# Two weight subtractions moved into the gating chain, and GpSimd's table products paced by the block, in the feed-forwards of a hybrid decoder

## Chip, cores and metric

The kernel runs on one core of one Trainium2 chip. The metric is the device time of one launch in microseconds (us).

## What is computed

A decoder trunk of two layers over 256 positions of width 1024, all in float32. Each layer adds half a feed-forward, a token mixer and half a second feed-forward to `x`; a last RMSNorm ends it.

```python
def swiglu(h, w_gate, w_up, w_down):
    return (jax.nn.silu(h @ w_gate) * (h @ w_up)) @ w_down

for l in range(2):
    x = x + 0.5 * swiglu(rmsnorm(x, norm_w[l, 0]), ffn_w_gate[l, 0], ffn_w_up[l, 0], ffn_w_down[l, 0])
    h = rmsnorm(x, norm_w[l, 1])
    m = even_mixer(h, ...) if l % 2 == 0 else odd_mixer(h, ...)
    x = x + m
    x = x + 0.5 * swiglu(rmsnorm(x, norm_w[l, 2]), ffn_w_gate[l, 1], ffn_w_up[l, 1], ffn_w_down[l, 1])
return rmsnorm(x, final_norm_w)
```

The hidden width of a feed-forward is 2816, that is 22 blocks of 128. The even mixer is spatial gating beside sparse attention; the odd mixer is causal pooling beside a diagonal state-space layer, for which tables (powers of a complex number, products of them with the matrices B and C, phases) have to be made from the parameters. There are four feed-forwards, called f = 0 to 3 here; the even mixer stands between 0 and 1, the odd one between 2 and 3.

## The kernel before

Products in float32 are made from two halves: a tile is rounded to `fp32r` (the high half, `h`) and the rest is kept as the low half (`l`), and three matmuls add high x high, low x high and high x low. The weights come as a stream of units of 128 x 1024 in the order in which TensorE wants them. One `raw` load on SP's queue (L87) brings two units; for each unit ScalarE makes `wh` (L97) and VectorE makes `wl`, the rest (L98). Three `raw` buffers and seven pairs `wh`, `wl` rotate. `used()` tells that a unit is done with and splits further units (`split_to`) up to six ahead; a further load is issued behind the subtraction that frees its buffer (`load_to`).

A feed-forward (`ffn(f)`) works block by block. For block j, `proj` multiplies the two units of gate and up weights into the PSUM bank `gu[j]` (48 matmuls, L125, L127, L132), and `chain(j)` makes the gated product: VectorE scales it (`e`, L252), ScalarE takes the silu (`s`, L255), VectorE multiplies (`h`, L257), ScalarE rounds (`hh`, L260), VectorE keeps the rest (`hl`, L261). `down(j)` multiplies one unit of down weights by `hh` and `hl` into the four banks `y` (24 matmuls, L114 to L116: the first two need `hh`, the third `hl`).

The order on every engine is the order of the program; nothing reorders it. Blocks 0 to 2 are opened together (`opening`); from j = 3 on a block is `proj(j)`, `chain(j)`, `down(j-1)`, and after the loop `down(21)` stands alone, with the update of `x` and the preparation of the next stage (`done`, L738 and `xprep2`, `xlow`) behind it. As `used()` is called twice within `proj`, VectorE's order in a block is `wl`, `wl`, `e`, `h`, `hl`, and one more `wl` after `down`.

`jobs[f, j]` holds work for the mixers that is issued ahead of block j. For the odd mixer (`odd_prep`), f = 0 has small operations of 32 to 288 columns on GpSimd; f = 1 and the start of f = 2 have the products `mul2`, each three GpSimd operations of 512 columns (L923 to L925), one `mul2` a block: two for `bbar` and eight for `wtw` in blocks 3 to 12 of f = 1, two scalings and the load of `cq` in block 13, five for `vt` in blocks 14 to 18, and four in blocks 3 to 6 of f = 2. `turn_w` (four TensorE transposes and a copy by ScalarE) needs all of `wtw` and `cols` and `taps` need `vt`. `bounce` brings a table through DRAM by DMAs on GpSimd's queue (`kd`, `toep`), and `phase` makes the phases in blocks 15 to 18 of f = 2. A copy of one column of `hl[2]` into `pace` (L289) holds GpSimd back until the first loop block of f = 0, 1 and 2; behind it GpSimd runs through its queue as fast as it can.

Of the kernel before, what the change touches and what calls it, by code (L numbers as in the profile page):

```python
# [7 lines left out]
F32 = mybir.dt.float32  # L8
# [4 lines left out]
OP = mybir.AluOpType  # L13
# [8 lines left out]
AHEAD = 6  # L22
# [35 lines left out]
def trunk(ctx, tc, a, out):  # L58
# [12 lines left out]
    def bank(i, name):  # L71
        return ps.tile([128, 512], F32, tag=f"bank{i}", name=name)

    v2 = lambda t: t.rearrange("p (a b) -> p a b", a=2)
    V, S, P, G = nc.vector, nc.scalar, nc.tensor, nc.gpsimd
# [2 lines left out]
    where = {u: i for i, u in enumerate(units)}  # L78
    nchunk = len(units) // 2
    raw, halves = {}, {}  # L80
    at = {"load": 0, "split": 0, "used": 0, "hold": False}

    def load_to(n):
        while at["load"] < min(n, nchunk):
            c = at["load"]
            raw[c] = wts.tile([128, 2, 1024], F32, tag="raw", name="raw", bufs=3)
            nc.sync.dma_start(raw[c], a["ws"][c].rearrange("p (u n) -> p u n", u=2))  # L87
            at["load"] += 1

    def split_to(n):  # L90
        while at["split"] < min(n, len(units)):
            i = at["split"]
            load_to(i // 2 + 1)
            src = raw[i // 2][:, i % 2]
            h = wts.tile([128, 1024], F32R, tag="wh", name="wh", bufs=AHEAD + 1)
            lo = wts.tile([128, 1024], F32R, tag="wl", name="wl", bufs=AHEAD + 1)
            S.copy(h, src)  # L97
            V.tensor_tensor(lo, src, h.bitcast(F32), op=OP.subtract)  # L98
            halves[i] = (h, lo)
            at["split"] += 1  # L100
            load_to((i + 1) // 2 + 3)

    def unit(u):
        i = where[u]
        assert i <= at["used"] + AHEAD and i < at["split"], (u, i, at)
        return halves[i]

    def used(n=1):
        at["used"] += n
        if not at["hold"]:  # L110
            split_to(at["used"] + AHEAD)
# [6 lines left out]
    def pairs(todo, half, ks=range(4)):  # L118
        for k in ks:
            for name, o in todo:  # L120
                h, lo = unit(("w", name, half))
                for s in range(2):
                    c = slice(256 * k + 128 * s, 256 * k + 128 * s + 128)
                    os = o[:, T * s:T * s + T]
                    P.matmul(os, h[:, c], xh[:, 4 * half + k], start=half == 0 and k == 0 and s == 0, stop=False,  # L125
                             skip_group_check=True)
                    P.matmul(os, lo[:, c], xh[:, 4 * half + k], start=False, stop=False, skip_group_check=True)  # L127
            for name, o in todo:
                h, lo = unit(("w", name, half))
                for s in range(2):  # L130
                    c = slice(256 * k + 128 * s, 256 * k + 128 * s + 128)
                    P.matmul(o[:, T * s:T * s + T], h[:, c], xl[:, 4 * half + k], start=False,  # L132
                             stop=half == 1 and k == 3, skip_group_check=True)

    def opening(todo, extra=None):
        at["hold"] = False
        split_to(5 if extra else at["used"] + AHEAD)
        n = 4 if extra else 1
        pairs(todo, 0)
        pairs(todo, 1, range(n))  # L140
        stats()
        used(2)
        pairs(todo, 1, range(n, 4))
        if extra:
            pairs([extra], 0)
        spread()

    def proj(name, o):
        pairs([(name, o)], 0)
        used()  # L150
        pairs([(name, o)], 1)
        used()
# [86 lines left out]
    def rows_out(u, y, ah, al, first, last, done=None):  # L239
        h, lo = unit(u)  # L240
        for d in range(ND):
            c = slice(128 * d, 128 * d + 128)
            mm3(y[d // 2][:, T * (d % 2):T * (d % 2) + T], h[:, c], lo[:, c], ah, al, first and d % 2 == 0, last)
            if done and d % 2:
                done(d // 2, y[d // 2])

    def ffn(f, after):
        gu, hh, hl, y = {}, {}, {}, {}

        def chain(j):  # L250
            e = v2(wk.tile([128, 512], F32, tag="e", name="e", bufs=3))
            V.tensor_tensor(e, gu[j].rearrange("p (a b) -> p a b", a=2), rb[:, None, :].to_broadcast([128, 2, T]),  # L252
                            op=OP.mult)
            s = wk.tile([128, T], F32, tag="s", name="s")
            S.activation(s, e[:, 0], AF.Silu)  # L255
            h = wk.tile([128, T], F32, tag="h", name="h")
            V.tensor_tensor(h, s, e[:, 1], op=OP.mult)  # L257
            hh[j] = wk.tile([128, T], F32R, tag="hh", name="hh", bufs=3)
            hl[j] = wk.tile([128, T], F32R, tag="hl", name="hl", bufs=3)
            S.copy(hh[j], h)  # L260
            V.tensor_tensor(hl[j], h, hh[j].bitcast(F32), op=OP.subtract)  # L261

        def down(j, done=None):
            if j == 0:
                for i in range(4):
                    y[i] = bank(i, "y")
            rows_out(("d", f, j), y, hh[j], hl[j], j == 0, j == NM - 1, done)

        for j in range(2):
            gu[j] = bank(4 + j, "gu")  # L270
        gu[2] = bank(6, "gu")
        extra = None if f else ((f, 2), gu[2])
        opening([((f, j), gu[j]) for j in range(2)], extra)
        chain(0)
        chain(1)
        used(2)
        if not extra:
            pairs([((f, 2), gu[2])], 0)
        used()
        pairs([((f, 2), gu[2])], 1)  # L280
        used()
        chain(2)
        down(0)
        used()
        down(1)
        used()
        for j in range(3, NM):
            if j == 3 and f < 3:
                G.tensor_copy(pace, hl[j - 1].bitcast(F32)[:, 0:1])  # L289
            for job in jobs.get((f, j), ()):  # L290
                job()
            gu[j] = bank(4 + j % 3, "gu")
            proj((f, j), gu[j])
            chain(j)
            down(j - 1)
            used()
        down(NM - 1, after)
        used()
# [415 lines left out]
    for half in range(2):  # L714
        for u in (2 * half, 2 * half + 1):
            halves[u] = tuple(wts.tile([128, 1024], F32R, tag=t, name=t, bufs=AHEAD + 1) for t in ("wh", "wl"))
        for k in range(4):
# [4 lines left out]
            for u in range(2):  # L722
                c = slice(256 * k, 256 * k + 256)
                h, lo = halves[2 * half + u]
# [33 lines left out]
    def odd_prep():  # L758
# [147 lines left out]
        def put(f, j0, per, todo):  # L906
            for i, t in enumerate(todo):
                jobs.setdefault((f, j0 + i // per), []).append(t)
# [40 lines left out]
        def turn_w(q):  # L949
            p = bank(7, "wt")  # L950
            for n in range(4):
                P.transpose(p[:, 128 * n:128 * n + 128], tw["w"][:, 4 * q + n].rearrange("p c i -> p (c i)"), ident)
            S.copy(uu[:, 4 * q:4 * q + 4], p.rearrange("p (a b) -> p a b", a=4))
# [6 lines left out]
        def taps(r4):  # L960
            kc = tw[r4]
            if r4 % 2 == 0:
                tw["p"] = bank(7, "kt")
            p = tw["p"].rearrange("p (r e n) -> p r e n", r=2, e=2)
            for e in range(2):
                for q in range(4):
                    g = 2 * (4 * r4 + q)
                    P.matmul(p[32 * q:32 * q + 32, r4 % 2, e], bbar[:, 0, g:g + 2].rearrange("p g c -> p (g c)"),
                             kc[:, 2 * q + e].rearrange("p n c -> p (n c)"), start=True, stop=True,
                             skip_group_check=True)  # L970
            if r4 % 2:
                S.copy(kk[:, :, r4 - 1:r4 + 1].rearrange("p e r n -> p r e n"), p)
# [51 lines left out]
            f(w[:, :, 0:n], e[:, :, 1:m], bc(c), MUL)  # L1024
            f(e[:, :, m + 1:2 * m], u[:, :, 0:n], w[:, :, 0:n], ADD)

        put(1, 13, 1, [lambda q=q: turn_w(q) for q in range(8)])
        put(2, 8, 1, [lambda r=r: taps(r) for r in range(4)] + [diag, bounce, phase_open])
        put(2, 7, 1, [lambda r=r: cols(r) for r in range(4)])
        put(2, 15, 1, [lambda m=m: phase(m) for m in (2, 4, 8, 16)])  # L1030
# [209 lines left out]
            run(g_)  # L1240

    jobs = {}
    tw = {}
    prm = cst.tile([128, 3, 32], F32, name="prm")
    sgn = cst.tile([128, 1], F32, name="sgn")
# [4 lines left out]
    for t_, n_ in ((prm, "prm"), (sgn, "sgn")):  # L1250
        nc.gpsimd.dma_start(t_, a[n_])
    prep = odd_prep()
    next(prep)
    ffn(0, step(1, 0.5))
    even(step(2, 1.0))
    evp_cm.__exit__(None, None, None)
# [17 lines left out]
    odd_open()  # L1274
    next(prep, None)
    ffn(1, step(3, 0.5))
    ffn(2, step(4, 0.5))
    odd(step(5, 1.0))
    ovp_cm.__exit__(None, None, None)
# [20 lines left out]
    for h2 in (1, 0):  # L1300
        for t in range(2):
            n = 2 * t + h2
# [157 lines left out]
```

## Time and profile before

| | |
|---|---|
| median of 3 runs | 996.04 us (995.7 to 997.96) |
| the profiled execution | 998.27 us, span 996.6 us |
| TensorE matmuls busy | 963.1 us, 97% of the span |
| VectorE, ScalarE, GpSimd busy | 69%, 49%, 31% |
| granted clock of TensorE, mean | 0.988 |

The span is the time from the first to the last instruction of the profiled execution. The feed-forwards lie at about 24 to 200 us (f = 0), 331 to 531 us (f = 1), 531 to 724 us (f = 2) and 795 to 985 us (f = 3). Matmuls are pipelined and the ends of their records are modelled, so their start times are what tells when TensorE waited.

### The profile page before, as it was taken

Reading aid. Unit: us, or ns where it says so; the run is one execution under the profiler, and the core shown is the slowest. Engines: PE = TensorE matmul, PEld = TensorE weight load, DVE = VectorE, ACT = ScalarE, POOL = GpSimd, SP = SyncE. Lnnn points to the kernel's source line nnn. Section 1 sums busy time; section 2 is a strip of 40 time slices with the busy share of each in tenths; the row PEclk is TensorE's granted clock in tenths of the full one; section 3 lists DMA queues with packets and bytes.
Section 4 is the critical chain, followed back from the end, with each engine's and each line's share of the span. In section 5 each row is a group of like instructions: output and inputs, shape, how many; then the busy total and the mean of one; then the engine's idle time right before and its main releaser. Section 6 shows DMA issues by size and latency. Waiting matters only on the chain.

```text
span 996.6 us, 19296 instructions
## 1 busy us (share of the span) xinstructions
PE 963.1 (97%) x8075; PEld 938.1 (94%) x8075; DVE 685.2 (69%) x943; ACT 484.6 (49%) x741; POOL 310.8 (31%) x439
## 2 busy tenths in 40 slices
PE   8999999998788999999999999999999999999997
PEld 7999999997677998899999999999998999999997
DVE  6766666597755788886558875658687687566663
ACT  6544444477444553445544444434454655444442
POOL 1399989010020259860001622296010000000001
PEclk9999999999889999999999999999999999999998
DMA  7665664533212544546443464595543546545521
GB/s 259 254 223 183 231 234 178 211 134 141 107 43 85 182 170 173 190 177 243 167 172 127 179 233 176 197 254 194 187 134 127 206 150 231 207 175 185 196 86 43
DMA packets 32856, 175.47 MB, mean 176 GB/s; under 512 B 7792, under 2 KB 10032, under 8 KB 12928
## 3 DMA queue, kind: packets, MB, share of 16 engines
q1 hardware_dynamic: 29696, 166.21, 46.2%
q0 software_dynamic: 2496, 7.41, 2.7%
q8 instruction: 63, 1.03, 0.4%
q10 hardware_dynamic: 576, 0.62, 0.2%
q14 instruction: 25, 0.20, 0.1%
HBM read 172.12 MB, written 2.10 MB: 175 GB/s over the span
## 4 chain that ended last, share of the span: by engine, by line
PE 78%; DVE 11%; ACT 4%; issue 4%; POOL 1%; DMA 1%; SPq 1%; ACTq 0%; POOLq 0%; DVEq 0%
PE gu L125 14%; PE gu L127 14%; PE gu L132 14%; PE y L116 8%; PE y L114 8%; PE y L115 8%; DVE wl L98 5%; DVE h L257 1%; ACT wh L97 1%; DVE e L252 1%; ACT pr L545 1%; DMA raw<-in_ws 1%; ACT s L255 1%; DVE pr L557 1%; PE ms L219 1%
## 5 line engine op out<-in xcount | busy, mean ns | idle before, releaser
L98 DVE TENSOR_TENSOR wl<-raw,wh 128x1024 fp32r<-128x1024 f32 x308 | 399.1, 1330 | 116.7 <-ACT wh L97 116.4
L125 PE MATMUL gu<-xh,wh 128*128 128x256 f32 x1408 | 365.6, 282 | 1.4 <-ACT wh L725 1.4
L127 PE MATMUL gu<-xh,wl 128*128 128x256 f32 x1408 | 364.3, 282 | 0.6 <-DVE wl L726 0.4
L97 ACT CAST wh<-raw 128x1024 fp32r<-128x1024 f32 x308 | 310.4, 1048 | 92.0 <-PE gu L132 42.7
L132 PE MATMUL gu<-xl,wh 128*128 128x256 f32 x1408 | 275.9, 281 | 0.0
L125 PEld LDWEIGHTS gu<-xh,wh 128*128 128x128 f32 x1408 | 266.0, 189 | 3.0 <-ACT wh L725 2.1
L127 PEld LDWEIGHTS gu<-xh,wl 128*128 128x128 f32 x1408 | 265.1, 188 | 2.0 <-DVE wl L726 1.7
L132 PEld LDWEIGHTS gu<-xl,wh 128*128 128x128 f32 x1408 | 213.7, 188 | 0.0
L114 PE MATMUL y<-hh,wh 128*128 128x256 f32 x704 | 198.4, 282 | 4.6 <-ACT hh L260 4.6
L116 PE MATMUL y<-hl,wh 128*128 128x256 f32 x704 | 199.0, 283 | 1.5 <-DVE hl L261 1.5
L115 PE MATMUL y<-hh,wl 128*128 128x256 f32 x704 | 198.3, 282 | 0.0
L255 ACT ACTIVATE s<-e 128x256 f32<-128x256 f32 x88 | 36.8, 418 | 240.1 <-DVE e L252 240.1
L114 PEld LDWEIGHTS y<-hh,wh 128*128 128x128 f32 x704 | 132.6, 188 | 5.8 <-ACT hh L260 5.8
L116 PEld LDWEIGHTS y<-hl,wh 128*128 128x128 f32 x704 | 132.5, 188 | 3.0 <-DVE hl L261 2.9
L115 PEld LDWEIGHTS y<-hh,wl 128*128 128x128 f32 x704 | 132.6, 188 | 0.0
L197 POOL TENSOR_TENSOR sq<-sq 128x512 f32<-128x512 f32 x10 | 13.7, 1366 | 255.9 <-ACT sq L195 187.8
L252 DVE TENSOR_TENSOR e<-gu,rb 128x512 f32<-128x512 f32 x88 | 60.5, 688 | 31.7 <-PE gu L132 30.7
L257 DVE TENSOR_TENSOR h<-s,e 128x256 f32<-128x256 f32 x88 | 47.9, 544 | 48.3 <-ACT s L255 48.3
L261 DVE TENSOR_TENSOR hl<-h,hh 128x256 fp32r<-128x256 f32 x88 | 41.2, 468 | 41.7 <-ACT hh L260 41.7
L260 ACT CAST hh<-h 128x256 fp32r<-128x256 f32 x88 | 35.8, 407 | 53.7 <-DVE h L257 53.7
L747 POOL TENSOR_SCALAR sq<-x,gw 128x256 f32<-128x256 f32 x4 | 3.6, 917 | 184.2 <-DVE x L738 184.2
L775 POOL TENSOR_TENSOR sq<-sq 128x64 f32<-128x64 f32 (+1 forms) x120 | 59.5, 515 | 3.6
(334 smaller groups left out, 1134.5 us busy)
## 6 DMA issues: line engine op xcount, KB each, us to landing
raw<-in_ws SPq DMA_DIRECT2D x154, 1024.0 KB, 4.8
toep<-kd POOLq DMA_DIRECT2D x8, 256.0 KB, 8.4
raw<-in_ws SPq DMA_DIRECT2D x4, 256.0 KB, 4.0
raw<-in_ws SPq DMA_DIRECT2D x2, 512.0 KB, 8.0
w<-in_w POOLq DMA_DIRECT2D x1, 1024.0 KB, 5.2
bnd<-in_bnd POOLq DMA_DIRECT2D x1, 544.0 KB, 5.4
x<-in_x SPq DMA_DIRECT2D x4, 128.0 KB, 3.3
x<-in_x SPq DMA_DIRECT2D x2, 256.0 KB, 7.3
```

Source lines behind the costliest of these rows:

```text
L97: S.copy(h, src)
L98: V.tensor_tensor(lo, src, h.bitcast(F32), op=OP.subtract)
L114: P.matmul(o, h, ah, start=first, stop=False, skip_group_check=True)
L115: P.matmul(o, lo, ah, start=False, stop=False, skip_group_check=True)
L116: P.matmul(o, h, al, start=False, stop=last, skip_group_check=True)
L125: P.matmul(os, h[:, c], xh[:, 4 * half + k], start=half == 0 and k == 0 and s == 0, stop=False, skip_group_check=True)
L127: P.matmul(os, lo[:, c], xh[:, 4 * half + k], start=False, stop=False, skip_group_check=True)
L132: P.matmul(o[:, T * s:T * s + T], h[:, c], xl[:, 4 * half + k], start=False, stop=half == 1 and k == 3, skip_group_check=True)
L252: V.tensor_tensor(e, gu[j].rearrange("p (a b) -> p a b", a=2), rb[:, None, :].to_broadcast([128, 2, T]), op=OP.mult)
L255: S.activation(s, e[:, 0], AF.Silu)
L257: V.tensor_tensor(h, s, e[:, 1], op=OP.mult)
L775: steps.append(lambda: G.tensor_tensor(o, p, q, op=op))
```

## The change

Within `proj` of the loop blocks (j from 3 on) the subtraction `wl` isn't issued with its `wh` any more but noted in `lows`. `chain(j)` issues one of the two behind the silu, ahead of `h`, and one behind `hh`, ahead of `hl`; what is left is issued after the chain. `load_to` goes with the subtraction. ScalarE's order stays. The copy into `pace` is issued ahead of the jobs of more blocks: block 3 of f = 0 as before, blocks 3 to 18 of f = 1, and blocks 3 to 6 and 15 to 18 of f = 2. `turn_w` starts at block 14 instead of 13.

```diff
@@ split_to @@
             S.copy(h, src)
-            V.tensor_tensor(lo, src, h.bitcast(F32), op=OP.subtract)
             halves[i] = (h, lo)
             at["split"] += 1
+            lows.append((i, src, h, lo))
+            if not at["wait"]:
+                lower()
+
+    def lower(n=None):
+        while lows and n != 0:
+            i, src, h, lo = lows.pop(0)
+            V.tensor_tensor(lo, src, h.bitcast(F32), op=OP.subtract)
             load_to((i + 1) // 2 + 3)
+            n = n and n - 1
...
@@ chain @@
             S.activation(s, e[:, 0], AF.Silu)
+            lower(1)
             h = wk.tile([128, T], F32, tag="h", name="h")
             V.tensor_tensor(h, s, e[:, 1], op=OP.mult)
...
             S.copy(hh[j], h)
+            lower(1)
             V.tensor_tensor(hl[j], h, hh[j].bitcast(F32), op=OP.subtract)
...
@@ ffn @@
         for j in range(3, NM):
-            if j == 3 and f < 3:
+            if (f, j) in paced:
                 G.tensor_copy(pace, hl[j - 1].bitcast(F32)[:, 0:1])
             for job in jobs.get((f, j), ()):
                 job()
             gu[j] = bank(4 + j % 3, "gu")
+            at["wait"] = True
             proj((f, j), gu[j])
+            at["wait"] = False
             chain(j)
+            lower()
             down(j - 1)
             used()
...
-        put(1, 13, 1, [lambda q=q: turn_w(q) for q in range(8)])
+        put(1, 14, 1, [lambda q=q: turn_w(q) for q in range(8)])
...
+    paced = {(0, 3)} | {(1, j) for j in range(3, 19)} | {(2, j) for j in (3, 4, 5, 6, 15, 16, 17, 18)}
```

## Rows read from the trace of the kernel before

**Rows 1.** The page: busy time of the engines (us, share of the span, instructions), and the issues of the weight loads (count, KB each, us from issue to landing).

```profile
PE 963.1 (97%) x8075; PEld 938.1 (94%) x8075; DVE 685.2 (69%) x943; ACT 484.6 (49%) x741; POOL 310.8 (31%) x439
...
raw<-in_ws SPq DMA_DIRECT2D x154, 1024.0 KB, 4.8
```

**Rows 2.** Busy time in windows of 25 us, in the order PE, PEld, DVE, ACT, POOL, each with its number of instructions, then the granted clock, the DMA share and GB/s: a window of f = 0 and two of f = 1.

```profile
75.00:100.00 25.00, 25.00 (x213) 25.00 (x212) 16.66 (x18) 11.33 (x15) 24.38 (x51) 1.00 0.52 184
...
375.00:400.00 25.00, 22.56 (x182) 21.54 (x180) 21.59 (x16) 8.07 (x12) 24.21 (x16) 1.00 0.50 180
400.00:425.00 25.00, 23.68 (x193) 23.08 (x194) 21.56 (x18) 10.80 (x15) 21.10 (x16) 1.00 0.53 196
```

**Rows 3.** Who waited for whom, TensorE only (us in total, times, longest): first in 345 to 440 us, then in 540 to 600 us.

```profile
PE y L114 <- ACT hh L260: 2.8, 4, 0.7
PE y L116 <- DVE hl L261: 1.2, 5, 0.3
...
PE y L114 <- ACT hh L260: 0.6, 1, 0.6
PE y L116 <- DVE hl L261: 0.4, 1, 0.4
```

**Rows 4.** Timeline of TensorE in f = 1 (start us, duration us, what; in brackets the idle time before it and what ended it): the beginning of the first and the fifth stalled `down`.

```profile
370.29 0.28 PE L114 MATMUL y<-hh,wh 128*128 128x256 f32 x1
...
370.86 0.39 PE L116 MATMUL y<-hl,wh 128*128 128x256 f32 x1 [0.17 <-DVE hl L261]
...
410.86 0.39 PE L116 MATMUL y<-hl,wh 128*128 128x256 f32 x1 [0.20 <-DVE hl L261]
```

**Rows 5.** The same in f = 2.

```profile
568.88 0.28 PE L114 MATMUL y<-hh,wh 128*128 128x256 f32 x1
...
579.05 0.39 PE L116 MATMUL y<-hl,wh 128*128 128x256 f32 x1 [0.38 <-DVE hl L261]
```

**Rows 6.** Timeline of VectorE in the stalled blocks of f = 1 (equal neighbours are merged, with their count).

```profile
358.95 8.07 DVE L98 TENSOR_TENSOR wl<-raw,wh 128x1024 fp32r<-128x1024 f32 x4 [0.53 <-ACT wh L97]
...
370.07 0.73 DVE L261 TENSOR_TENSOR hl<-h,hh 128x256 fp32r<-128x256 f32 x1 [0.47 <-ACT hh L260]
371.01 6.03 DVE L98 TENSOR_TENSOR wl<-raw,wh 128x1024 fp32r<-128x1024 f32 x3 [0.21 <-ACT wh L97]
...
378.19 1.43 DVE L257 TENSOR_TENSOR h<-s,e 128x256 f32<-128x256 f32 x1 [0.54 <-ACT s L255]
...
381.04 6.02 DVE L98 TENSOR_TENSOR wl<-raw,wh 128x1024 fp32r<-128x1024 f32 x3 [0.22 <-ACT wh L97]
```

**Rows 7.** Timelines of the last two blocks of f = 0: VectorE, then TensorE (the beginning of `down(21)`).

```profile
184.12 1.22 DVE L98 TENSOR_TENSOR wl<-raw,wh 128x1024 fp32r<-128x1024 f32 x1 [1.36 <-ACT wh L97]
185.83 0.69 DVE L252 TENSOR_TENSOR e<-gu,rb 128x512 f32<-128x512 f32 x1 [0.49 <-PE gu L132]
...
188.91 2.36 DVE L98 TENSOR_TENSOR wl<-raw,wh 128x1024 fp32r<-128x1024 f32 x2 [0.53 <-ACT wh L97]
...
194.36 0.69 DVE L252 TENSOR_TENSOR e<-gu,rb 128x512 f32<-128x512 f32 x1 [0.47 <-PE gu L132]
195.60 0.43 DVE L257 TENSOR_TENSOR h<-s,e 128x256 f32<-128x256 f32 x1 [0.55 <-ACT s L255]
196.50 0.42 DVE L261 TENSOR_TENSOR hl<-h,hh 128x256 fp32r<-128x256 f32 x1 [0.47 <-ACT hh L260]
...
198.59 0.68 DVE L738 SCALAR_TENSOR_TENSOR x<-y,x 128x512 f32<-128x512 f32 x1
...
197.01 0.28 PE L114 MATMUL y<-hh,wh 128*128 128x256 f32 x1
...
197.24 0.28 PE L116 MATMUL y<-hl,wh 128*128 128x256 f32 x1
```

**Rows 8.** Timeline of VectorE in a block of f = 2 without GpSimd.

```profile
585.59 3.50 DVE L98 TENSOR_TENSOR wl<-raw,wh 128x1024 fp32r<-128x1024 f32 x3 [0.45 <-ACT wh L97]
```

**Rows 9.** GpSimd in f = 1: timeline of the copy into `pace`, the first product, a short one, the last one for `wtw` and the last one for `vt`; then a group of its products in 358 to 440 us (count, busy us, mean ns, idle us before).

```profile
358.48 0.19 POOL L289 COPY pace<-hl 128x1 f32<-128x1 f32 x1 [19.63 <-DVE hl L261]
358.63 1.06 POOL L923 TENSOR_TENSOR gt<-bq,turn 128x512 f32<-128x512 f32 x1
...
390.52 1.24 POOL L924 TENSOR_TENSOR gt<-bbar,pw 128x512 f32<-128x512 f32 x1
...
408.10 1.30 POOL L925 TENSOR_TENSOR wtw<-gt 128x512 f32<-128x512 f32 x1
...
437.52 2.16 POOL L925 TENSOR_TENSOR vt<-gt 128x512 f32<-128x512 f32 x1
...
L925 POOL TENSOR_TENSOR wtw<-gt 128x512 f32<-128x512 f32 x8 | 13.9, 1737 | 0.6
```

**Rows 10.** The weight loads in f = 2: timeline of SP's queue (issues) and of ScalarE, and the landing times of the loads in 640 to 690 us.

```profile
647.33 0.33 SPq L87 DMA_DIRECT2D raw<-in_ws  x1
655.94 0.33 SPq L87 DMA_DIRECT2D raw<-in_ws  x1
...
660.93 1.99 ACT L97 CAST wh<-raw 128x1024 fp32r<-128x1024 f32 x2
668.05 1.05 ACT L97 CAST wh<-raw 128x1024 fp32r<-128x1024 f32 x1 [5.13 <-DMA raw<-in_ws]
...
DMA to landing us min/median/max: 4.7/6.2/12.0
```

More of the change, by code (lines that the diff above doesn't have):

```diff
@@ L80, in trunk @@
     raw, halves = {}, {}
-    at = {"load": 0, "split": 0, "used": 0, "hold": False}
+    at = {"load": 0, "split": 0, "used": 0, "hold": False, "wait": False}
+    lows = []
     def load_to(n):
@@ L97, in split_to @@
             S.copy(h, src)
-            V.tensor_tensor(lo, src, h.bitcast(F32), op=OP.subtract)
             halves[i] = (h, lo)
             at["split"] += 1
+            lows.append((i, src, h, lo))
[5 more added lines that the diff above has]
+            V.tensor_tensor(lo, src, h.bitcast(F32), op=OP.subtract)
             load_to((i + 1) // 2 + 3)
+            n = n and n - 1
     def unit(u):
         i = where[u]
-        assert i <= at["used"] + AHEAD and i < at["split"], (u, i, at)
+        assert i <= at["used"] + AHEAD and i < at["split"] - len(lows), (u, i, at)
         return halves[i]
```

## Prediction, made before the change was run

> **What bounds the kernel now.** I read the page's busy table first: TensorE's matmuls cover 97% of the span and VectorE 69% [rows 1]. An average hides where the missing part lies, so I went to the windows of 25 us [rows 2]. A window of a feed-forward in which TensorE never waits holds 213 matmuls (75 to 100 us). In the second feed-forward one holds 182 and one 193, and exactly there GpSimd is busy for 21 to 24 of 25 us and VectorE for 21.6; the granted clock is 1.00 throughout, so this isn't a slower TensorE but a waiting one. The list of who waited for whom says for what: in 345 to 440 us TensorE waits for `hh` and `hl`, the last two tiles of the gating chain, and in 540 to 600 us once more for each [rows 3].
>
> The start times give the loss exactly. A block (`proj(j)`, then `down(j-1)`) takes 8.53 us where TensorE sets the pace: `e` starts at 185.83 and 194.36 [rows 7]. The first stalled `down` starts at 370.29 and could have had its first matmul with `hl` 0.24 us later; that of the fifth starts at 410.86, where 370.53 + 4 x 8.53 = 404.65 would do [rows 4]: 6.2 us lost in the second feed-forward. In the third, 568.88 + 8.53 + 0.24 = 577.65 stands against 579.05 one block on: 1.4 us [rows 5]. Together **7.6 us**, and no change to this loop can win more there.
>
> Why is the chain late? VectorE's timeline [rows 6]: from one `wl` group at 371.01 to the next at 381.04 is 10.03 us, with three `wl` (6.03), `e`, `h` (1.43), `hl` (0.73) and three idle gaps of 0.54 + 0.47 + 0.22 = 1.23 us; so it is busy for 8.80 us of each block, and a block cannot take less than 10.03. Undisturbed, three `wl` in a row take 3.50 us and `h` and `hl` 0.43 [rows 7, 8]. The difference goes with GpSimd: its products run without a pause from 358.63 on, and those of L925 last 1.74 us in the mean where an undisturbed one has 1.30 [rows 9]. Both engines lengthen each other.
>
> **The change, part by part.**
>
> *(a) Two `wl` go into the chain.* VectorE's order in a block was `wl`, `wl`, `e`, `h`, `hl`, `wl`; it becomes `e`, `wl`, `h`, `wl`, `hl`, `wl`. No instruction is added. Where VectorE is behind, the two gaps (0.54 and 0.47 us) are filled: 1.0 us per block won. Where it is not behind (most blocks), the chain gets longer instead. The step from one VectorE start to the next with no wait between is 1.14 us for `wl` (2.36 - 1.22) [rows 7, 8]; for `h` I take 0.35 and for `e` 0.61, their durations less the same overlap of 0.08. From `e`'s start to `hl`'s end: 0.61 + 1.14 + 0.35 + 1.14 + 0.42 = 3.66 us, where 194.36 to 196.92 were 2.56 [rows 7]. In the loop that costs nothing: `hl` of block j is wanted only a whole block later (8.53 us), and that block hides it. The `wl` itself moves by up to 4.8 us (one block's second ends at 188.91 + 2.36 = 191.27; behind the `e` of 194.36 it ends at 196.11 [rows 7]), and is wanted two blocks later.
>
> The loads move with it, since a `raw` load leaves SP's queue only when the subtraction has freed its buffer. Five units lie between: the load issued at 647.33 feeds the `wh` at 660.93, 13.6 us later; 8.8 us remain after the change [rows 10]. Landing takes 4.8 us in the median of the page and 12.0 us once, beside the `toep` transfers [rows 1, 10]. That one is issued at 655.94 and already holds ScalarE until 668.05, without a wait of TensorE; it belongs to the third `wl` of a block, which moves by only 1.1 us. I take nothing: a landing of 12.0 us against the 8.8 left would bring a `wh` 3.2 us late, and TensorE wants it only two blocks on; should ScalarE's wait hold the chain instead, 3.2 us is the bound.
>
> *(b) The last block of a feed-forward.* Here the cover is gone: after `proj(21)` only `down(20)` stands before the `down(21)` that wants this very `hl`. Before, `hl` ends at 196.92 and the matmul that needs it starts at 197.24: 0.32 us to spare [rows 7]. With 3.66 us it ends at 198.02, the matmul follows 0.06 us later (as 370.07 + 0.73 and 370.86 show [rows 4, 6]): 198.08 - 197.24 = **0.84 us of stall**. `hh` ends at 196.98 and is in time for 197.01. The first three feed-forwards have this, as units of the next stage are still being split; the fourth has none left to split. 3 x 0.84 = **2.5 us**. TensorE opens the next stage at once, so nothing takes it back; the `x` update behind it moves by less (last `wl` from 197.60 + 0.35 = 197.95 on, `x` at 199.09 and not 198.59 [rows 7]: 0.5 us), so 3 x 0.5 = 1.5 us is the low bound. That `wl` lasts 1.22 us where a wait precedes it gives the high one: 3 x 1.0 = 3.0 us.
>
> [...]
>
> *(c) GpSimd's products paced.* Each paced block puts a copy of one column (0.19 us [rows 9]) ahead of that block's jobs; it waits for the `hl` of the block before, and all later GpSimd work queues behind it: the products, the load of `cq`, the copies of `cols`; `turn_w` and `taps` on TensorE wait for those (d). One block then has three products; so far the ten `mul2` of blocks 3 to 12, 30 products, ran from 358.63 to 409.40 [rows 9], that is 5.9 per 10.03 us. What do three cost? VectorE's undisturbed block is 0.61 + 3 x 1.14 + 0.35 + 0.42 = 4.80 us, so 3.73 us of 8.53 are to spare. From the contended block, (8.80 - 4.80) / 5.9 = 0.68 us per product, three 2.0 us; at most their whole undisturbed length, 1.06 + 1.24 + 1.30 = 3.6 us [rows 9]. Both fit: no paced block has VectorE as its bound, and as the products start with `hl`'s end, most fall into VectorE's idle time before the next `e`. So I take **all 7.6 us** as won; kept back are at worst the first stalls of each feed-forward, 370.53 to 370.86, 0.3 us each. The first loop block has four `wl` (8.07 us from 358.95 [rows 6]); two now follow `e`, which can start near 363.0 instead of behind all four. So `hl` ends, with every operation as long as under products (0.61 + 2.01 + 1.43 + 2.01 + 0.73), by 369.8, against 370.53.
>
> [...]
>
> *(d) Later needs.* The tables end later (358.5 + 15 x 8.53 + 3.6 = about 490 us instead of 439.7 [rows 9]); `turn_w` starts one block later, a whole block after its last product, and its eight blocks are as long at 14 to 21 as at 13 to 20. In the third feed-forward the last product ends near the end of block 6, `taps` needs it at block 8. Nothing.
>
> **Sum.** -7.6 + 2.5 = -5.1 us. The profiled execution took 998.27 us (span 996.6); it would become 993.2 and the span 991.5. It lies 2.2 us above the median of the runs, 996.04; against that I forecast 990.9, **991 us**.
>
> **Rivals.**
> 1. *The tail costs nothing* (the copy `hh` or the queue hides it, or the next stage takes it back): 996.0 - 7.6 = 988.4. Against it: only 0.32 us to spare. Chance 0.08.
> 2. *Half of the stalls stay*, because products meet the longer chain where `wl`, `h` and `hl` now stand in a row: each paced block then pays somewhat, -3.8 + 2.5: 994.7. For it: `h` at 1.43 us under products. Chance 0.13.
> 3. [...] GpSimd does the same products, and if each holds VectorE wherever it falls, the lost 7.6 us come back spread over the paced blocks, and the tails are added: 996.0 + 2.5 = 998.5. It decides from 3.73 / 3 = 1.24 us of VectorE per product on; the rows give 0.68 on average, and 1.0 for `h`. Chance 0.07.
> 4. *The change does nothing*: late `raw` loads hold `wh`, then `s` and the whole chain behind it, and take as much as is won: 996. For it only the one landing of 12.0 us. Chance 0.05.
>
> **How the numbers follow.** The forecast has 0.67, with its own range 989.5 to 993 (tails 1.5 to 3.0, 0.6 of stalls kept, and the runs' own scatter). Two in ten left out give 988.0 to 995.5, which takes in rivals 1 and 2. What tells from no change is 0.2%, 2.0 us, so "faster" ends at 994.05: the forecast, rival 1 and a third of rival 2, 0.79; same 0.13; slower 0.08.
>
> **What would show it.** TensorE's waits for `hh` and `hl` between 345 and 600 us gone, 213 matmuls in each window less the transposes; three new waits for `hl` of about 0.8 us at the ends of the first three feed-forwards; between `e` and `h` a `wl` and no idle; GpSimd's products in groups of three with pauses. Wrong would be: `wl` still near 2.0 us in all three places of a block, TensorE waits in paced blocks after 440 us, or ScalarE's `wh` waiting for `raw`.

## The result and the profile after

The changed kernel takes 991.42 us (median of 4 runs, 990.87 to 992.38), the kernel before beside it 996.9 us (4 runs, 995.7 to 997.96): the ratio is 0.9944 with a 95% interval of [0.9932, 0.9956], 4.4 to 6.8 us less. The forecast was 991.0. The time came out as foretold, and the stalls went where they were expected to go; but the experiments show that one of the two halves of the change, the new order, does nearly all of it alone, while the prediction had rested the claim that all 7.6 us go on the other, the pacing. That it hit to 0.4 us is in part luck: it counted 5.1 us down from a median of 996.04, and 5.5 us were measured from 996.9. Lines of `kernel.py` are nine to fourteen further on now: `wl` is L108, `e` L261, `s` L264, `h` L267, `hh` L270, `hl` L272, `pace` L300, `down` L123 to L125, the products L937 to L939.

The busy table and two groups of the page of the changed kernel (count, busy us, mean ns, idle time before), to be held against [rows 1]:

```profile
PE 959.7 (97%) x8075; PEld 936.7 (95%) x8075; DVE 631.5 (64%) x943; ACT 485.4 (49%) x741; POOL 294.0 (30%) x461
...
L108 DVE TENSOR_TENSOR wl<-raw,wh 128x1024 fp32r<-128x1024 f32 x308 | 382.0, 1252 | 14.9 <-ACT wh L98 14.9
...
L300 POOL COPY pace<-hl 128x1 f32<-128x1 f32 x25 | 25.0, 1001 | 151.5 <-DVE hl L272 151.5
```

VectorE has as many instructions as before and is busy for 53.7 us less; GpSimd has 22 more (the copies into `pace`) and is busy for 16.8 us less all the same. So less time is lost between these two. The windows of f = 1 in the same columns as [rows 2] show what TensorE got of it: 214 matmuls where there were 182 and 193, and VectorE and GpSimd busy for little over half of the time.

```profile
375.00:400.00 25.00, 25.00 (x214) 25.00 (x213) 14.29 (x18) 11.34 (x15) 13.14 (x12) 1.00 0.50 184
400.00:425.00 25.00, 25.00 (x214) 25.00 (x213) 13.84 (x19) 10.92 (x15) 12.93 (x13) 1.00 0.52 189
```

Who waited for whom, TensorE only, from 345 to 600 us; this is all that is left of [rows 3], and it is the tail of f = 1:

```profile
PE y L125 <- DVE hl L272: 0.5, 1, 0.5
```

A paced block on VectorE, then on GpSimd (start us, duration us, what; in brackets the idle time before it and what ended it):

```profile
386.80 0.69 DVE L261 TENSOR_TENSOR e<-gu,rb 128x512 f32<-128x512 f32 x1 [3.72 <-PE gu L141]
387.41 1.22 DVE L108 TENSOR_TENSOR wl<-raw,wh 128x1024 fp32r<-128x1024 f32 x1
388.54 0.42 DVE L267 TENSOR_TENSOR h<-s,e 128x256 f32<-128x256 f32 x1
388.88 1.22 DVE L108 TENSOR_TENSOR wl<-raw,wh 128x1024 fp32r<-128x1024 f32 x1
390.01 0.42 DVE L272 TENSOR_TENSOR hl<-h,hh 128x256 fp32r<-128x256 f32 x1
390.39 1.23 DVE L108 TENSOR_TENSOR wl<-raw,wh 128x1024 fp32r<-128x1024 f32 x1
395.33 0.69 DVE L261 TENSOR_TENSOR e<-gu,rb 128x512 f32<-128x512 f32 x1 [3.71 <-PE gu L141]
```

```profile
390.50 1.16 POOL L300 COPY pace<-hl 128x1 f32<-128x1 f32 x1 [3.95 <-DVE hl L272]
391.62 1.06 POOL L937 TENSOR_TENSOR gt<-bbar,pw 128x512 f32<-128x512 f32 x1
392.64 1.06 POOL L938 TENSOR_TENSOR gt<-bbar,pw 128x512 f32<-128x512 f32 x1
393.77 1.30 POOL L939 TENSOR_TENSOR wtw<-gt 128x512 f32<-128x512 f32 x1
```

The gaps between `e`, `h` and `hl` are filled, a block of VectorE is 4.82 us (386.80 to 391.62), and the three products lie wholly in VectorE's idle time, each as long as an undisturbed one.

Where the time went, stage by stage. The table is worked out from the start times of `e`: from the first `e` of a feed-forward to that of its last block, and from that to the first `e` of the next feed-forward, which holds the tail and, after f = 0 and f = 2, a mixer. The last four columns belong to the experiments.

| us | before | changed | order only | pace only | old tail | behind chain |
|---|---|---|---|---|---|---|
| f = 0, first `e` to last | 167.46 | 167.46 | 167.47 | 167.45 | 167.51 | 167.53 |
| f = 1 | 180.02 | 173.56 | 173.89 | 177.11 | 173.57 | 174.67 |
| f = 2 | 174.70 | 173.18 | 173.19 | 173.18 | 173.19 | 173.19 |
| f = 3 | 170.12 | 170.13 | 170.12 | 170.13 | 170.13 | 170.13 |
| tail of f = 1, next opening | 18.56 | 19.25 | 19.25 | 18.56 | 18.57 | 20.21 |
| tail of f = 2, odd mixer | 90.82 | 91.45 | 91.37 | 91.13 | 90.86 | 92.89 |
| tail of f = 0, even mixer | 150.97 | 149.68 | 149.89 | 149.26 | 149.00 | 152.51 |

The stalls removed are 6.46 (f = 1) + 1.52 (f = 2) = 7.98 us. Two tails cost 0.69 and 0.63 us; the third is hidden in the even mixer, whose time differs by 1.55 us between two executions of the very same changed kernel (149.68 here, 151.23 in the repeat below), so that profiled spans alone can't be compared to a microsecond. If the third is taken like the other two, which is an estimate, the gain by the stages is some 6.0 us; the runs give 5.5, within 4.4 to 6.8.

### The profile page after: what moved, and what is told of

Same layout as the page of the kernel before. It is cut to its first block, busy times and chain, and to the rows that moved or that the text cites. A ratio compares the mean times of both kernels' runs of the same rounds, so it can differ in the third digit from the quotient of the medians.

```text
span 989.2 us, 19297 instructions
## 1 busy us (share of the span) xinstructions
PE 959.7 (97%) x8075; PEld 936.7 (95%) x8075; DVE 631.5 (64%) x943; ACT 485.4 (49%) x741; POOL 294.0 (30%) x461
## 4 chain that ended last, share of the span: by engine, by line
PE 87%; DVE 6%; ACT 2%; issue 2%; DMA 1%; POOL 1%; SPq 1%; ACTq 0%; POOLq 0%; DVEq 0%
PE gu L134 16%; PE gu L136 16%; PE gu L141 16%; PE y L125 9%; PE y L124 9%; PE y L123 9%; DVE wl L108 2%; DMA raw<-in_ws 1%; ACT pr L559 1%; DVE pr L571 1%; PE ms L228 0%; PE sc L547 0%; PE glu L125 0%; PE zc L164 0%; PE zd L134 0%
## 5 line engine op out<-in xcount | busy, mean ns | idle before, releaser
L108 DVE TENSOR_TENSOR wl<-raw,wh 128x1024 fp32r<-128x1024 f32 x308 | 382.0, 1252 | 14.9 <-ACT wh L98 14.9
L261 DVE TENSOR_TENSOR e<-gu,rb 128x512 f32<-128x512 f32 x88 | 60.8, 690 | 256.9 <-PE gu L141 255.7
L125 PE MATMUL y<-hl,wh 128*128 128x256 f32 x704 | 198.6, 282 | 1.6 <-DVE hl L272 1.6
L123 PE MATMUL y<-hh,wh 128*128 128x256 f32 x704 | 198.2, 282 | 1.2 <-ACT hh L270 1.2
L264 ACT ACTIVATE s<-e 128x256 f32<-128x256 f32 x88 | 36.8, 418 | 204.4 <-DVE e L261 204.3
L125 PEld LDWEIGHTS y<-hl,wh 128*128 128x128 f32 x704 | 132.5, 188 | 2.4 <-DVE hl L272 2.4
L123 PEld LDWEIGHTS y<-hh,wh 128*128 128x128 f32 x704 | 132.6, 188 | 1.6 <-ACT hh L270 1.4
L270 ACT CAST hh<-h 128x256 fp32r<-128x256 f32 x88 | 35.8, 407 | 85.5 <-DVE h L267 85.5
L300 POOL COPY pace<-hl 128x1 f32<-128x1 f32 x25 | 25.0, 1001 | 151.5 <-DVE hl L272 151.5
L789 POOL TENSOR_TENSOR sq<-sq 128x64 f32<-128x64 f32 (+1 forms) x120 | 53.3, 463 | 3.6
L267 DVE TENSOR_TENSOR h<-s,e 128x256 f32<-128x256 f32 x88 | 39.4, 448 | 8.2 <-ACT s L264 8.2
```

Source lines behind the costliest of these rows:

```text
L123: P.matmul(o, h, ah, start=first, stop=False, skip_group_check=True)
L125: P.matmul(o, h, al, start=False, stop=last, skip_group_check=True)
L789: steps.append(lambda: G.tensor_tensor(o, p, q, op=op))
```

## Experiments

**The changed kernel once more.** No edit.

> The changed kernel itself once more, as the measure for the other three on the same chip: 5.1 to 5.5 us below before by the sum and by the first runs.

Measured: 991.49 us (990.07 to 991.92), ratio 0.9943 [0.9931, 0.9954]; f = 1 took 173.57 us, f = 2 173.18.

**The order alone.** The subtractions stay in the chain, the pacing is taken out, and `turn_w` starts at block 13 as before.

```diff
-        put(1, 14, 1, [lambda q=q: turn_w(q) for q in range(8)])
+        put(1, 13, 1, [lambda q=q: turn_w(q) for q in range(8)])
...
-    paced = {(0, 3)} | {(1, j) for j in range(3, 19)} | {(2, j) for j in (3, 4, 5, 6, 15, 16, 17, 18)}
+    paced = {(0, 3), (1, 3), (2, 3)}
```

> Only the new order of VectorE's queue: the two subtractions stand in the chain, but GpSimd is held back once per feed-forward, as before. My theory (both parts remove stalls, the tails cost 2.5 us): the two idle gaps of 1.0 us per stalled block go, VectorE's contended block falls from 10.03 to about 8.8 us against TensorE's 8.53, so some 0.3 us per block are kept over five to nine blocks, 1.5 to 2.5 of the 7.6 us; with the three tails the time is 2.6 to 3.6 us below before. Rival (pacing alone removes the stalls, the order only costs): 0 to 3 us above before. Rival (the order alone does it all): 5.1 us below before, as the whole change.

Measured: 991.49 us (990.18 to 992.16), ratio 0.9945 [0.9934, 0.9957]: as fast as the whole change. My theory missed (2.6 to 3.6 us below before), and its second rival, that the order alone does it all, came true. f = 1 keeps 0.33 us of its stalls, f = 2 none. VectorE, one block of f = 1 and the next `e`; then the window of 375 to 400 us:

```profile
379.72 0.68 DVE L261 TENSOR_TENSOR e<-gu,rb 128x512 f32<-128x512 f32 x1
380.32 1.48 DVE L108 TENSOR_TENSOR wl<-raw,wh 128x1024 fp32r<-128x1024 f32 x1
381.73 1.28 DVE L267 TENSOR_TENSOR h<-s,e 128x256 f32<-128x256 f32 x1
382.93 2.33 DVE L108 TENSOR_TENSOR wl<-raw,wh 128x1024 fp32r<-128x1024 f32 x1
385.18 1.28 DVE L272 TENSOR_TENSOR hl<-h,hh 128x256 fp32r<-128x256 f32 x1
386.38 2.08 DVE L108 TENSOR_TENSOR wl<-raw,wh 128x1024 fp32r<-128x1024 f32 x1
388.39 0.68 DVE L261 TENSOR_TENSOR e<-gu,rb 128x512 f32<-128x512 f32 x1
```

```profile
375.00:400.00 25.00, 25.00 (x212) 24.90 (x211) 25.00 (x18) 10.41 (x14) 24.29 (x15) 1.00 0.49 171
```

The sign that the prediction named as wrong is there in two of a block's three places, `wl` above 2 us; `h` and `hl` take 1.28, VectorE has no pause, GpSimd is as dense as before, and a block of VectorE is longer than TensorE's 8.53 us (five from 361.94 to 406.19: 8.85 each). And yet TensorE loses a third of a microsecond in all. An engine that falls behind by 0.3 us in each block need not cost 0.3 us in each block.

**The pacing alone.** VectorE's old order, everything else as changed.

```diff
-            at["wait"] = True
+            at["wait"] = False
```

> Only the pacing: VectorE's old order (two subtractions, e, h, hl, one subtraction), GpSimd's products wait for the preceding block's hl. Theory: no longer chain, so no stalls at the tails; a paced block costs VectorE 4.80 + 1.0 (gaps) + 2.0 to 3.0 (three products) = 7.8 to 8.8 us against 8.53, so most of the 7.6 us is won and 0 to 2 kept: 5.6 to 7.6 us below before, that is as fast as the whole change or up to 2.5 us faster. Rival (the order is needed, pacing only spreads the stalls): 0 to 3 us below before.

Measured: 992.61 us (992.3 to 993.09), ratio 0.9958 [0.9946, 0.997], 4.2 us below the kernel before: less than my theory expected (5.6 to 7.6) and more than the rival (0 to 3). f = 2 is free of stalls, f = 1 keeps 177.11 - 173.56 = 3.55 us, and TensorE doesn't wait for `hl` at the end of f = 1 (345 to 545 us), whose tail is 18.56 us as before. VectorE in f = 1, and the waits of TensorE's weight loads in 345 to 545 us (us in total, times, longest):

```profile
391.69 0.68 DVE L261 TENSOR_TENSOR e<-gu,rb 128x512 f32<-128x512 f32 x1
...
394.77 6.12 DVE L108 TENSOR_TENSOR wl<-raw,wh 128x1024 fp32r<-128x1024 f32 x3 [0.46 <-ACT wh L98]
400.82 0.68 DVE L261 TENSOR_TENSOR e<-gu,rb 128x512 f32<-128x512 f32 x1
```

```profile
PEld y L125 <- DVE hl L272: 1.4, 6, 0.2
PEld y L123 <- ACT hh L270: 1.3, 5, 0.3
```

In the old order three `wl` stand right behind `hl`, where the pacing puts the three products: 6.12 us instead of 3.50 [rows 8], so (6.12 - 3.50) / 3 = 0.87 us of VectorE per product, and 9.13 us per block (391.69 to 400.82). Pacing spreads the products but drives them onto the subtractions; it needs the new order to have them in idle time.

**The old order in the last block of each feed-forward**, the rest as changed.

```diff
-            at["wait"] = True
+            at["wait"] = j < NM - 1
```

> The whole change, but in block 21 of each feed-forward the subtractions keep their old place ahead of e. Theory: the three stalls of about 0.8 us ahead of the last down go and nothing else changes: 2.4 us faster than the changed kernel, 7.6 us below before, and no wait of TensorE for hl at the ends of the first three feed-forwards. Rival (the next stage takes the stall back): the same time as the changed kernel within 0.5 us.

Measured: 989.0 us (6 runs, 987.34 to 991.84), ratio 0.9925 [0.991, 0.9939], by the medians 2.5 us below the changed kernel measured beside it, by the means 1.8 (989.35 and 991.13): the runs scatter by more than that difference. TensorE has no wait for `hl` any more, and the two tails that can be read are back at 18.57 and 90.86 us, 0.68 and 0.59 us less.

**Order without pacing, old tail.** Both edits of "the order alone" and the one above.

> The new order of VectorE without the pacing (the copy into `pace` stands ahead of block 3 alone, `turn_w` at block 13 as before), and the last block of each feed-forward in its old order. Theory (a late chain costs TensorE nothing until the slack is used; the order alone holds the lateness below it): second feed-forward from its first `e` to its last 173.9 us, the third 173.2, no wait for `hl` at the ends; the time within 0.5 us of the kernel with pacing and the old tail, 989.0. Rival (pacing is worth something of its own where the tails are gone): over 1 us longer than that.

Measured: 989.78 us (6 runs, 988.87 to 990.91), ratio 0.9925 [0.9912, 0.9938], the same ratio as with pacing. f = 1 took 173.85 us, f = 2 173.19. The pacing is worth 0.3 us here, less than the runs can tell. These two kernels have the lowest medians, below the kernel before and, by the two tails in their traces too, below the changed one.

**All three subtractions behind the chain.** VectorE's order is `e`, `h`, `hl`, `wl`, `wl`, `wl`: `e` no longer stands behind two subtractions, but the chain's gaps stay empty. No pacing, `turn_w` at block 13.

```diff
             S.activation(s, e[:, 0], AF.Silu)
-            lower(1)
...
             S.copy(hh[j], h)
-            lower(1)
```

> All three subtractions of a block behind its chain (order `e`, `h`, `hl`, `wl`, `wl`, `wl`), so that `e` no longer stands behind two of them but the gaps of the chain stay empty; no pacing, `turn_w` at block 13. Theory A (what counts is how late `e` and `hl` are against their block, and the lag may grow to a slack before TensorE waits): blocks beside products take about 9.8 us, the lag grows 1.3 us a block against a slack of about 5 us, so 2 to 3 us of the 6.5 come back in the second feed-forward (first `e` to last `e` 175.5 to 176.5 us against 173.56), none in the third (173.2), no wait for `hl` at the ends; about 990 to 992 us in all. Theory B (the filled gaps are what counts): the gaps are as empty as before, so the second feed-forward stays at 179 to 180 us and the time at 995 or more.

Measured: 996.07 us (10 runs), ratio 0.9984 [0.9973, 0.9994]: the total is where theory B had it, and theory A's 990 to 992 us missed; but f = 1 took 174.67 us, so of the 6.46 us of stalls only 1.11 are left, and f = 2 has none, as theory A had the stages. VectorE from the first loop block's `e` on, then TensorE: its first matmul after `proj(3)`, the one after `proj(7)`, and the first that waits for `hl` in f = 1, in the `down` one block later:

```profile
364.16 0.68 DVE L261 TENSOR_TENSOR e<-gu,rb 128x512 f32<-128x512 f32 x1
...
383.15 0.68 DVE L261 TENSOR_TENSOR e<-gu,rb 128x512 f32<-128x512 f32 x1
384.37 1.44 DVE L266 TENSOR_TENSOR h<-s,e 128x256 f32<-128x256 f32 x1 [0.54 <-ACT s L264]
386.35 0.66 DVE L270 TENSOR_TENSOR hl<-h,hh 128x256 fp32r<-128x256 f32 x1 [0.54 <-ACT hh L269]
386.94 6.32 DVE L108 TENSOR_TENSOR wl<-raw,wh 128x1024 fp32r<-128x1024 f32 x3
393.18 0.68 DVE L261 TENSOR_TENSOR e<-gu,rb 128x512 f32<-128x512 f32 x1
...
403.20 0.68 DVE L261 TENSOR_TENSOR e<-gu,rb 128x512 f32<-128x512 f32 x1
```

```profile
363.23 0.28 PE L123 MATMUL y<-hh,wh 128*128 128x256 f32 x1
...
397.34 0.28 PE L123 MATMUL y<-hh,wh 128*128 128x256 f32 x1
...
407.11 0.39 PE L125 MATMUL y<-hl,wh 128*128 128x256 f32 x1 [0.26 <-DVE hl L270]
```

This is the run that settles the cause. The block is as slow as before the change, 10.03 us (383.15 to 393.18) with the same gaps of `h` and `hl` and an `h` of 1.44 us (1.43 in [rows 6]), and still five sixths of the loss are gone. What differs is where it starts from: block after block `e`, `h`, `hl`, `wl`, `wl`, `wl` is the same round as before, begun at another place. In the kernel before, the first contended `e` came behind four `wl` (TensorE's first matmul after `proj(3)`, then that `e`):

```profile
361.77 0.28 PE L114 MATMUL y<-hh,wh 128*128 128x256 f32 x1
```

```profile
366.94 0.68 DVE L252 TENSOR_TENSOR e<-gu,rb 128x512 f32<-128x512 f32 x1
```

`proj(3)` was done by 361.77 and `e` began at 366.94: 5.17 us late. `hl` is wanted at 370.53 (the prediction's working), 8.76 us after `proj(3)`; from `e` to the end of `hl` are 3.86 us (366.94 to 370.80 [rows 6]) and 0.06 to the matmul, so `e` may be 8.76 - 3.86 - 0.06 = 4.84 us late at no cost; this is the slack, and how late `e` stands is the lag. It was 0.33 us beyond that from the first block on, and each further contended block paid its 1.5 us in full. With the subtractions behind the chain the first `e` is 0.93 us late (363.23 to 364.16); four blocks later `proj` is done by 397.34 and `e` begins at 403.20, 5.86 us late, 1.02 beyond 4.84, and the matmul stands at 407.11 where 397.34 + 8.76 = 406.10 would have done: 1.01 us.

The slack is not the same in every order, for it shrinks as the chain gets longer. With the order alone the chain beside products takes 6.74 us, from `e` at 379.72 to the end of `hl` at 386.46, which leaves 8.76 - 6.74 - 0.06 = 1.96; `e` is 0.93 us late at first and 2.38 five blocks later (403.81 to 406.19), only 0.42 beyond the slack, so little is lost. With the pacing alone the chain is 2.62 us (391.69 to 394.31) and the slack 6.08; the first `e` is already 4.29 us late (360.23 to 364.52), the lag grows by about 0.6 a block and stands at 6.49 at the fifth `e` (394.33 to 400.82): from there on each block pays, and the next six (394.33 to 448.63) lose 54.30 - 6 x 8.53 = 3.12 of its 3.55 us.

That this kernel isn't faster has another place: at the end of a feed-forward three `wl` stand ahead of the update of `x`, and the tails take 20.21 and 92.89 us, 1.65 and 2.07 more than before. At the end of f = 1 TensorE has no wait for `hl`; it waits 1.50 us for the next stage's input `xh` (its matmuls start at 526.84 and then at 528.62).

**Twice the work for GpSimd.** Each operation of the products is done twice with the same values, once with the order alone and once with the whole change; `turn_w` starts at block 17, two in a block, in both.

```diff
-            G.tensor_tensor(t, f1, wide(s1), op=OP.mult)
-            G.tensor_tensor(u, f2, wide(s2), op=OP.mult)
-            G.tensor_tensor(o, t, u, op=op)
+            for _ in range(2):
+                G.tensor_tensor(t, f1, wide(s1), op=OP.mult)
+                G.tensor_tensor(u, f2, wide(s2), op=OP.mult)
+                G.tensor_tensor(o, t, u, op=op)
```

> The new order without pacing, and each of the three operations of every product of two complex factors done twice with the same values, so that GpSimd has twice the work; `turn_w` starts at block 17, two in a block. Theory A (a block beside products is 8.87 us against TensorE's 8.53, 0.34 us more; TensorE waits only for what goes beyond about 1.9 us of slack): twice as many contended blocks let the lag reach some 4 to 5 us, so the second feed-forward takes 2 to 3.5 us more than the 173.9 of the single products: 176 to 177.5 us; the third at most 0.5 more than 173.2. Theory B (no lag is carried, the contended block never costs TensorE anything in the new order): 173.9 again.

> The whole change with the pacing, and each operation of the products done twice, six per paced block instead of three; `turn_w` at block 17, two in a block. The idle time of VectorE behind the last `wl` is about 3.7 us and holds three products of 1.06 us; six don't fit. Theory A (pacing helps only as long as a block's products fit into that idle time): three of the six meet the `wl` and `h` of the next block, GpSimd comes near to a whole block (3 x 1.06 + 3 x 2.04 + 0.2 = 9.5 us), so it runs nearly without a pause and the second feed-forward is within 1 us of the unpaced run with doubled products. Theory B (pacing spreads the work, whatever its amount): 173.6 us, 2 us or more below the unpaced one.

Measured: 1013.08 us and 1006.8 us (2 runs each); f = 1 took 189.18 and 182.42 us, f = 2 178.84 and 181.25, so the figures that the expectations gave for both stages missed. These totals don't answer the question. Two `turn_w` in a block make TensorE wait for ScalarE's copies between them (us in total, times, longest; 475 to 545 us, without pacing, then with it), and in f = 2 the block with the first `taps`, whose tables GpSimd now has later, takes 13.47 and 17.39 us from `e` to `e`, where the changed kernel has 9.29. I had foreseen neither:

```profile
PE wt L967 <- ACT uu L968: 8.1, 4, 2.6
```

```profile
PE wt L967 <- ACT uu L968: 5.6, 3, 2.6
```

Ahead of `turn_w` the question has an answer. From the first `e` of f = 1 to that of block 16, TensorE's own pace is 101.90 us to block 13, read from the changed kernel, and 3 x 8.53 on: 127.49 us. Without pacing it is 129.46 (1.97 us of stalls), with it 127.49 (none). So stalls return when the lag has time to grow, as the slack would have it (theory A of the first had 2 to 3.5 us for it), and pacing then takes them away, against my theory A of the second: it was to help only while a block's products fit into the idle time, and six don't. One window of each, without pacing, then with it, shows how narrow that is; VectorE has a little idle time again, GpSimd works almost without a pause in both.

```profile
400.00:425.00 25.00, 24.79 (x206) 24.32 (x205) 25.00 (x18) 11.04 (x15) 24.29 (x15) 1.00 0.48 170
```

```profile
400.00:425.00 25.00, 25.00 (x213) 25.00 (x212) 24.55 (x19) 10.51 (x15) 24.53 (x17) 1.00 0.49 176
```

From one `e` to the next are 8.50 us there (mean of eight from block 4 on), which is TensorE's pace, and 8.80 without pacing. Whether that difference of at least 0.3 us comes from the copies into `pace`, which put about a microsecond between the products of two blocks, isn't told by these runs.

## Why the prediction was right, and where it wasn't

*What bounds the kernel: right.* 7.6 us were read as the loss, 6.2 in f = 1 and 1.4 in f = 2; 6.46 and 1.52 were removed. TensorE's own pace leaves no more to win in this loop: f = 1 takes f = 3's 170.13 us and eight `turn_w` of 0.43 us (a block with one is 8.96 us), 173.57, and 173.56 were measured.

*(a) Filled gaps: right in size, wrong in weight.* Two gaps of 1.0 us per block were to be won; the contended block went from 10.03 to 8.85 us. But the order alone was expected to leave 1.5 to 2.5 us of the stalls, and it left 0.33; and the old block under pacing was expected to leave 0 to 2, and it left 3.55. The step that failed is the reading of a block that "cannot take less than 10.03" as a loss of 1.5 us in each such block. It is one only when the slack is used up. What the part (c) noted in passing, that `e` of the first loop block no longer stands behind four `wl`, was the main effect: the first `e` stands 4.2 us earlier (5.17 us late before, 0.94 after: `proj(3)` is done by 361.02 there and `e` begins at 361.96, the first two rows below), and what that leaves is only just used up by the few contended blocks of the order alone. Of the 6.46 us in f = 1, `e` ahead of the subtractions gives 5.35, the filled gaps 0.8, the pacing 0.3, if they are added in this order; put in first, the pacing takes away 2.91 (180.02 to 177.11), so these shares hold for this order alone. The loads went as expected: the longest landing in 630 to 690 us was 12.4 us (12.0 before [rows 10]); it held VectorE's `wl` for 3.47 us, TensorE not at all, so rival 4 had nothing. The rows are of TensorE and VectorE in the first loop block, of the weight loads' landing, and of VectorE behind the late load:

```profile
361.02 0.28 PE L123 MATMUL y<-hh,wh 128*128 128x256 f32 x1
...
361.96 0.68 DVE L261 TENSOR_TENSOR e<-gu,rb 128x512 f32<-128x512 f32 x1
```

```profile
DMA to landing us min/median/max: 4.6/5.0/12.4
```

```profile
658.00 1.23 DVE L108 TENSOR_TENSOR wl<-raw,wh 128x1024 fp32r<-128x1024 f32 x1 [3.47 <-ACT wh L98]
```

*(b) The tail: right at the matmul, somewhat too dear behind it.* 0.84 us of stall in three places were foretold. VectorE and TensorE at the end of f = 0, to be held against [rows 7]:

```profile
194.91 0.69 DVE L261 TENSOR_TENSOR e<-gu,rb 128x512 f32<-128x512 f32 x1 [3.72 <-PE gu L141]
...
198.12 0.42 DVE L272 TENSOR_TENSOR hl<-h,hh 128x256 fp32r<-128x256 f32 x1
```

```profile
198.59 0.39 PE L125 MATMUL y<-hl,wh 128*128 128x256 f32 x1 [0.53 <-DVE hl L272]
```

From `e` to that matmul are 3.68 us, where 2.88 were: 0.80. To the next stage's `e` 0.63 to 0.69 of it remain, so that nothing takes it back is not quite so; three such tails are about 2.0 us, an estimate, as the third can't be read. With the old tail the runs give 2.5 us back by their medians and 1.8 by their means, so rival 1 falls, but that the medians show just the 2.5 of the sum is chance.

*(c) Pacing: the outcome right, the credit wrong.* Three products were taken at 0.68 us of VectorE each, at most 1.24. In the changed kernel they cost it nothing (4.82 us against 4.80 undisturbed), with the old order 0.87. Rival 2 (half of the stalls stay) came true for the pacing alone (3.55 of 7.98 us stay), not for the change; rival 3 (each product holds VectorE wherever it falls) is refuted by the busy table: VectorE has 53.7 us of busy time less and GpSimd 16.8, for the same products. That the two lengthen each other is visible, though, where both run without a pause.

With the order alone `wl` takes 2.08 to 2.33 us beside products in two of a block's three places, and `h` and `hl` 1.28 (379.72 to 388.39), where the paced block of the changed kernel has 1.22 or 1.23 and 0.42; `e`, which reads `gu`, takes 0.68 or 0.69 in every kernel. The operations of the `wtw` products last 1.51, 1.64 and 1.74 us in the mean in the kernel before and 1.06, 1.06 and 1.31 in the changed one (L923 to L925, then L937 to L939, 358 to 440 us). What makes `e` different isn't shown by these runs. In the paced block the third `wl` starts first, at 390.39; the copy begins at 390.50 and the first product at 391.62, as that `wl` ends.

*(d) Later needs: right.* The last `vt` product ends at 490.6 us (490 foretold), without a wait of `turn_w` or `taps`.

## What to carry to other kernels

When an engine beside the bottleneck needs longer for a block than the bottleneck does, don't multiply the excess by the blocks: read how late its first operation already stands, how late its result may come, and compare the growth with what is left; here a loss that seemed to be one of rate was for five sixths one of a late start, which had used up the slack at once. In an in-order queue, put work that is wanted two blocks later behind the start of the chain that is wanted one block later, and leave that order out where the next thing waits for the chain's own end, as in the last block: here some 2 us for three such places. And undo each half of a change by itself, for a right total is no evidence for its parts, and the parts need not add up.

## What was not expected of the hardware

The copy of one column into `pace` takes 1.16 us where it follows VectorE's `hl` with a `wl` already under way, 0.19 where VectorE is idle [rows 9]: from 390.50 to 391.66, while that `wl` ran from 390.39 to 391.62. In this trace the copy lasted until the subtraction that it met had ended, and held GpSimd's queue for that long; so it is with 21 of the 25 copies (1.08 to 1.17 us, each over 0.03 to 0.06 us after its `wl`), while the other four, which met no instruction of VectorE, took 0.18 or 0.19.
